# Parts of the output projection's operand in DRAM, and attention as one evenly spaced sequence with TensorE in source order

## The chip, the cores and the metric

The kernel runs on one core of a Trainium2 chip. The metric is the device time of one execution in microseconds (us), as the median of several runs. Profiles show one execution each; their times count from the start of its span.

The engines, as the profile names them: PE is TensorE (matmuls; PEld its weight loads), DVE is VectorE, ACT is ScalarE, POOL is GpSimd, SP is SyncE, which here only issues DMAs. ACT issues some DMAs and POOL issues others.

## What is computed

One block of a hybrid model on 512 tokens of width 2048, all in float32: a normalisation, one wide input projection, two mixers side by side (a state-space mixer, SSD, and a sparse attention with three branches), an output projection over both mixers' outputs, and a gated feed-forward net.

```python
u = rmsnorm(h, attn_norm_w)
z, xbc, dt, q, kc, vc, ks, vs, kw, vw, gate = split(u @ w_in)
y_ssd = rmsnorm(ssd(xbc, dt) * silu(z), ssd_norm_w)        # 1024 columns
# attention, 4 groups of 4 heads with 64 columns each; 1024 columns
o = g0 * softmax(q @ k_cmp) @ v_cmp                        # compressed branch
  + g1 * softmax(q_rot @ ks) @ vs + g2 * softmax(q_rot @ kw) @ vw
h = h + concat(y_ssd, o) @ w_out
h = h + (silu(n @ w_gate) * (n @ w_up)) @ w_down           # n = rmsnorm(h)
```

At 512 tokens both other branches reach over all earlier tokens, so the kernel computes them as two plain causal softmaxes with their own keys and values.

## The kernel before

All operands of matmuls are split into a high part in a short float format (`fp32r`) and a low part, the rest: `a_hi` makes the high part on ACT, `lo` the low part on DVE. A product takes three matmuls: high by high, high by low, low by high. Data stand transposed: features on the 128 partitions, the 512 tokens along the free dimension.

**Units.** Input and output projection are a list of units. A unit is one block of 128 output columns: it loads its weights in pieces of four k blocks (`raw` ring, SP's queue), splits them three pieces ahead (`whi` on ACT, `wlo` on DVE, rings of four), and runs three matmuls of 512 columns for each k block against the operand `U` (16 blocks of high parts, 16 of low parts), into `ps_g`. An input unit has 16 k blocks, an output unit 8 to 12: `NS` says how many, and the rest of the output projection is done later (the "oa" steps, lines 1184 to 1186). After its last matmul a unit's result is worked on by its evacuation, a generator `ev_...`.

**The order.** `Sched` holds generators. Each k block of a unit ends with `sch.tick()`, one step; `yield 3` in a generator means that it goes on three steps later. So everything that is not a projection (evacuations, attention, loads for the next stage) is written in between the units' matmuls, at distances counted in steps. `run_until` steps on without projection matmuls until a flag is set. From this source order the compiler makes each engine's own order: outside `manual_schedule` it may move instructions on TensorE ahead of or behind others by its own timing; inside, TensorE's instructions stay in source order. The other engines' order is the compiler's throughout. Before the change `manual_schedule` begins with the first unit of the output projection, `units[NU]`.

**Units of the second half of the input projection.** The z units (`U_Z`, eight; the evacuation multiplies the SSD mixer's result by silu(z) and stores the product in DRAM, `gy_d`), and for each attention group g the units VS, KS and two q units. Before, the order is VS0, KS0, Q00, Q01, Z4, Z5, VS1, KS1, Q10, Q11, Z6, VS2, KS2, Q20, Q21, Z7, VS3, KS3, Q30, Q31; then come the output units OUT0 to OUT15.

- `ev_vs` transposes the values on TensorE (line 698, tile `vt` into `ps_m`) and copies them into `v`, of which there are two; a third group waits until group g - 2 is finished, flag `("a", g - 2)`.
- `ev_ks` rotates the keys and makes `kh` and `kl`, two buffers each.
- `ev_q` makes `uq` (ACT and POOL), computes the compressed branch's scores (lines 776 and 777, into `ps_m`), and makes the rotated queries `rq`.
- `ps_m` is one PSUM bank, used by all of these in turn.

**Attention** is a generator of its own. For each group it waits for keys, values and both q units, does the compressed branch's softmax, and then goes through 32 items (4 heads, 2 branches, 4 blocks of queries). An item is `score` (two matmuls, a masked minimum on DVE, an exponential on ACT), `norm`, three items later `trans` (transposes, high and low parts `pth` and `ptl`), and after every fourth `pvmm`, the product with the values. An item takes one step and then `PACE` steps, 2.25 on the mean; from the output projection on `PACE_OUT`, 1.5. The first four blocks of 128 rows of attention's result are stored in DRAM as they are (`at_d`).

**Into the output projection.** The operand of the output projection takes the place of the input's in `U`. During the last input unit `ms_in` loads the SSD mixer's eight blocks from `gy_d`, multiplies them by the normalisation's row factor on POOL, and makes high and low part into `U`. At the first output unit `ma_in` loads attention's finished blocks, and splits them into `U`; the blocks that finish later are split into `U` directly. When attention is over, at the last output unit, `pre_oa` closes attention's pool and opens those of the next stage.

Of the kernel before, what the change touches and what calls it, by code (L numbers as in the profile page):

```python
# [29 lines left out]
PACE = [2,2,2,3]  # L30
PACE_OUT = [1,2,1,2]
LAG = 3
EB = 5
# [82 lines left out]
def body(ctx, tc, xT, w_in, w_out, w_gate, w_up, w_down, w1k, w1v, cols, rows, kst, out):  # L116
# [46 lines left out]
    at_d = dram.tile([8, 128, 512], F32, name="at_d")  # L163
# [384 lines left out]
    def ev_z(t):  # L548
        def ev(p):
# [33 lines left out]
    P2 = {}  # L583

# [103 lines left out]
    def ev_vs(g):  # L688
        def ev(p):
# [4 lines left out]
            yield 2  # L694
# [64 lines left out]
    def ev_q(g, j):  # L759
        def ev(p):  # L760
# [6 lines left out]
            yield 2  # L767
# [19 lines left out]
    def attention():  # L787
        yield from sch.wait("att", "cmp")
# [5 lines left out]
        for g in range(4):  # L794
            yield from sch.wait(("k", g), ("v", g), ("q", g, 0), ("q", g, 1))
            kh, kl = R["k", g]
            v = R["v", g]

            sc = R["sc", g]
            sm = ap.tile([128, 3, 4, 4], F32, tag="sm", name="sm", bufs=1)  # L800
            dve.tensor_reduce(sm[:, 0], sc, AX.X, ALU.max)
            dve.tensor_scalar(sm[:, 0], sm[:, 0], -1e20, None, op0=ALU.max)
            dve.tensor_tensor(sc.rearrange("p i h k -> p (i h) k"), sc.rearrange("p i h k -> p (i h) k"),
                              sm[:, 0].rearrange("p i h -> p (i h)")[:, :, None].to_broadcast([128, 16, 32]),
                              ALU.subtract)
            act.activation(sc, sc, AF.Exp, scale=0.125)
            for h in range(4):
                a_hi(vpad[32 * h:32 * h + 32, h, 0:64], vcmp[:, g, :])
                lo(dve, vpad[32 * h:32 * h + 32, h, 64:128], vcmp[:, g, :], vpad[32 * h:32 * h + 32, h, 0:64])
# [4 lines left out]
            mul(dve, sc.rearrange("p i h k -> p (i h) k"), sc.rearrange("p i h k -> p (i h) k"),  # L814
                sm[:, 2].rearrange("p i h -> p (i h)")[:, :, None].to_broadcast([128, 16, 32]))
            yield 6
            p = ps_t()
# [7 lines left out]
            yield 2  # L825

            items = [(h, br, i) for h in range(4) for br in range(2) for i in range(4)]
            pt, pr, po = {}, {}, {}

            def score(h, br, i):  # L830
                L = 128 * (i + 1)
                q = R["rq", g, h // 2][:, h % 2, i * 128:(i + 1) * 128]
                p = ps_s()
                pe.matmul(p[:, 0:L], q, kh[:, br, 0:L], start=True, stop=False)
                pe.matmul(p[:, 0:L], q, kl[:, br, 0:L], start=False, stop=True)
                e = ap.tile([128, 512], F32, tag="e", name="e", bufs=EB)
                m = ap.tile([128, 4], F32, tag="em", name="em", bufs=EB + 1)
                dve.tensor_tensor_reduce(e[:, 0:L], p[:, 0:L], kcs(K_AM + 512 - L, L), -0.125, 3e38,
                                         ALU.add, ALU.min, m[:, 0:1])
                act.activation(e[:, 0:L], e[:, 0:L], AF.Exp, scale=-1.0, bias=m[:, 0:1], accum_out=m[:, 1:2])  # L840
                pr[h, br, i] = (e, m)

            def norm(h, br, i):
                L = 128 * (i + 1)
                e, m = pr[h, br, i]
                gc = (4 * g + h) * 3 + 1 + br
                dve.reciprocal(m[:, 2:3], m[:, 1:2])
                if br:
                    dve.tensor_scalar(e[:, 0:L], e[:, 0:L], m[:, 2:3], gat[:, i, gc:gc + 1],
                                       op0=ALU.mult, op1=ALU.mult)  # L850
                else:
                    mul(dve, m[:, 3:4], m[:, 2:3], gat[:, i, gc:gc + 1])
                    a_hi(e[:, 0:L], e[:, 0:L], scale=m[:, 3:4])

            def trans(h, br, i):
                e, m = pr.pop((h, br, i))
                if i == 0:
                    pt[h, br] = (ap.tile([128, 13, 128], F32R, tag="pth", name="pth", bufs=2),
                                 ap.tile([128, 13, 128], F32R, tag="ptl", name="ptl", bufs=2))
                th, tl = pt[h, br]  # L860
                p = ps_t()
                for kb in range(i + 1):
                    pe.transpose(p[:, kb * 128:(kb + 1) * 128], e[:, kb * 128:(kb + 1) * 128], ident)
                s = p[:, 0:128 * (i + 1)].rearrange("p (a b) -> p a b", b=128)
                d = slice(i, 3 * i + i + 1, 3)
                a_hi(th[:, d, :], s)
                lo(dve, tl[:, d, :], s, th[:, d, :])

            def pvmm(h, br):
                th, tl = pt.pop((h, br))  # L870
                if br == 0:
                    o = po[h] = ps_v()
                    pe.matmul(o, vpad[:, h, :], ch, start=True, stop=False)
                    pe.matmul(o, vpad[:, h, :], cl, start=False, stop=False)
                o = po[h]
                for kb in range(4):
                    for t in (th, tl):
                        rhs = t[:, 4 * kb:3 * kb + 4, :].rearrange("p a b -> p (a b)")
                        pe.matmul(o[:, kb * 128:512], v[:, kb, br, :], rhs, start=False,
                                  stop=(br == 1 and kb == 3 and t is tl))  # L880
                if br == 1:
                    if h % 2 == 0:
                        R["at"] = ap.tile([128, 512], F32, tag="at", name="at", bufs=1)
                    at = R["at"]
                    a, b = (0, 64) if h % 2 == 0 else (64, 0)
                    fo = ap.tile([128, 512], F32, tag="fo", name="fo", bufs=1)
                    act.activation(fo[a:a + 64, :], o[b:b + 64, :], AF.Copy)
                    add(dve, at[a:a + 64, :], o[a:a + 64, :], fo[a:a + 64, :])
                    if h % 2:
                        k = 2 * g + h // 2  # L890
                        if "ma" in P2:
                            h_, l_ = P2["ma"][k]
                            a_hi(h_, at)
                            lo(dve, l_, at, h_)
                        else:
                            nc.gpsimd.dma_start(at_d[k], at)
                            P2["at"] = k
                        sch.flags.add(("at", k))

            n = len(items)  # L900
            for s in range(n + LAG + 1):
                if s < n:
                    score(*items[s])
                    if items[s][1:] == (1, 3):
                        sch.flags.add(("h", g, items[s][0]))
                yield 1
                if 0 <= s - LAG < n:
                    trans(*items[s - LAG])
                if s < n:
                    norm(*items[s])  # L910
                yield P2.get("pace", PACE)[s % len(PACE)]
                if 0 <= s - LAG - 1 < n and items[s - LAG - 1][2] == 3:
                    pvmm(*items[s - LAG - 1][:2])
            sch.flags.add(("a", g))
# [44 lines left out]
    def pre_ms():  # L959
        P2["ms"] = [(U[:, 0, k], U[:, 1, k]) for k in range(8)]  # L960
        sch.add(ms_in())

    def ms_in():
        assert "r2" in sch.flags
        for k in range(8):
            yield 2
            h_, l_ = P2["ms"][k]
            t = wp.tile([128, 512], F32, tag="raw", name="gy", bufs=4)
# [3 lines left out]
            dve.scalar_tensor_tensor(l_, t, col(C_SN + k), f(h_), op0=ALU.mult, op1=ALU.subtract)  # L972
            sch.flags.add(("ms", k))

    def pre_out():
        P2["pace"] = PACE_OUT
        sch.run_until(*[("gy", t) for t in range(8)])
        P2["ma"] = [(U[:, 0, 8 + k], U[:, 1, 8 + k]) for k in range(8)]
        sch.add(ma_in(P2["at"] + 1))

    def ma_in(n):

        for k in range(n):
            h_, l_ = P2["ma"][k]
# [4 lines left out]
            sch.flags.add(("ma", k))  # L989

    def ev_os(c):
        def ev(p):
            if c >= 12:
# [915 lines left out]
```

## Time and profile before

| | |
|---|---|
| three runs | 2238.38, 2241.39, 2245.98 us; median 2241.39 |
| the profiled execution | 2243.56 us, span 2241.8 us, mean granted clock of TensorE 0.986 |
| busy: PE, DVE, ACT, POOL | 97%, 80%, 53%, 19% of the span |
| second half of the input projection, from Q00's first matmul | 333.4 to 611.8 us |
| OUT0's first matmul | 631.8 us |
| attention's last matmul | 806.7 us |
| the end of the output units, and the first oa step | 823.3 us |

A row of the profile names the line of the code, the engine, the operation, the tiles written and read, the sizes, and how often; where time stands in brackets behind an arrow, the engine sat idle for that long before the instruction, and the arrow names what ended it. "PEclk" is the share of full speed that the throttle granted TensorE. Matmuls are pipelined, so the distance between two starts, not one's duration, is what a matmul costs.

### The profile page before, as it was taken

How to read it: one execution, taken by the hardware profiler on the slowest of the kernel's cores; microseconds unless marked ns; L12 is line 12 of the kernel's file. 1: busy time of each engine (PE TensorE's matmuls, PEld its weight loads, DVE VectorE, ACT ScalarE, POOL GpSimd, SP SyncE). 2: the span in 40 equal slices, each digit the busy share in tenths (PEclk: the TensorE clock that was granted, in tenths of full speed). 3: DMA queues.
4: the chain of work that ended last, by engine and by line, in shares of the span. 5: the costliest groups of instructions: out<-in, count | busy, mean ns of one | idle time of the engine just before them, and what ended most of it. 6: DMA issues, size and time to landing. Idle time of an engine off the chain costs nothing. (4 is left out here: it accounts for less than half of the span.)

```text
span 2241.8 us, 34995 instructions
## 1 busy us (share of the span) xinstructions
PE 2167.7 (97%) x12892; PEld 1908.6 (85%) x12892; DVE 1794.5 (80%) x2821; ACT 1196.4 (53%) x1991; POOL 432.3 (19%) x439
## 2 busy tenths in 40 slices
PE   7999999999999999999999999999999899999996
PEld 5888888888878887888888888888888889999996
DVE  7699766778886648988888888888887878888886
ACT  4564446666666657555555555555555333333453
POOL 2011225234331126000100000000000122221232
PEclk9999999999979999999999999999999999999998
DMA  5222343222334367788888788887878869686974
GB/s 179 90 71 76 120 151 100 76 83 69 97 88 116 104 189 226 223 222 251 227 228 235 219 249 231 239 235 214 249 218 268 315 197 307 191 283 183 298 184 135
DMA packets 170492, 416.66 MB, mean 186 GB/s; under 512 B 16800, under 2 KB 23984, under 8 KB 170320
## 3 DMA queue, kind: packets, MB, share of 16 engines
q1 hardware_dynamic: 98912, 246.73, 33.0%
q0 software_dynamic: 28112, 80.65, 18.4%
q10 hardware_dynamic: 43296, 87.04, 10.8%
q8 instruction: 101, 1.65, 0.3%
q14 instruction: 71, 0.58, 0.1%
HBM read 353.54 MB, written 57.15 MB: 183 GB/s over the span
## 5 line engine op out<-in xcount | busy, mean ns | idle before, releaser
L125 ACT ACTIVATE R<-Z 128x1024 fp32r<-128x1024 f32 (+4 forms) x458 | 415.5, 922 | 438.7 <-DVE Z L137 322.7
L128 DVE TENSOR_TENSOR R<-Z,R 128x1024 fp32r<-128x1024 f32 (+4 forms) x367 | 386.1, 1061 | 35.9 <-ACT R L125 21.1
L234 PE MATMUL ps_g<-u,whi 128*128 128x512 f32 x778 | 316.0, 406 | 0.0
L236 PE MATMUL ps_g<-u,wlo 128*128 128x512 f32 x778 | 307.7, 395 | 0.0
L235 PE MATMUL ps_g<-u,whi 128*128 128x512 f32 x778 | 306.3, 394 | 0.0
L1180 PE MATMUL ps_s<-u,R 128*128 128x512 f32 (+1 forms) x1160 | 252.9, 348 | 7.1 <-ACT A L1390 6.8
L128 DVE TENSOR_TENSOR wlo<-wraw,whi 128x512 fp32r<-128x512 f32 x211 | 159.5, 757 | 80.8 <-ACT whi L125 77.5
L1180 PEld LDWEIGHTS ps_s<-u,R 128*128 128x128 f32 x1160 | 187.7, 188 | 38.7 <-ACT A L1390 12.2
L125 ACT ACTIVATE whi<-wraw 128x512 fp32r<-128x512 f32 x211 | 131.9, 625 | 144.8 <-PE ps_g L235 98.6
L236 PEld LDWEIGHTS ps_g<-u,wlo 128*128 128x128 f32 x778 | 146.6, 188 | 30.6
L234 PEld LDWEIGHTS ps_g<-u,whi 128*128 128x128 f32 x778 | 147.0, 189 | 24.9 <-issue 0.2
L235 PEld LDWEIGHTS ps_g<-u,whi 128*128 128x128 f32 x778 | 147.1, 189 | 23.8
L1180 PE MATMUL ps_t<-u,R 128*128 128x512 f32 (+1 forms) x600 | 131.4, 347 | 0.0
L1180 PE MATMUL ps_g<-u,R 128*128 128x512 f32 x584 | 131.3, 349 | 0.0
L1180 PE MATMUL ps_s<-T,R 128*128 128x512 f32 (+1 forms) x560 | 125.7, 349 | 1.3 <-DVE R L128 1.3
L1180 PE MATMUL ps_g<-T,R 128*128 128x512 f32 (+1 forms) x584 | 125.7, 346 | 0.0
L1180 PE MATMUL ps_s<-V,R 128*128 128x512 f32 (+1 forms) x568 | 123.1, 347 | 0.0
L125 ACT ACTIVATE R<-A 128x1024 fp32r<-128x1024 f32 (+3 forms) x76 | 71.0, 934 | 86.3 <-DVE A L137 62.2
L137 DVE TENSOR_TENSOR Z<-Z 128x1024 f32<-128x1024 f32 (+5 forms) x96 | 106.1, 1105 | 8.8 <-POOL E L137 4.2
L137 DVE TENSOR_TENSOR A<-ps_g,A 128x512 f32<-128x512 f32 (+1 forms) x110 | 71.1, 653 | 51.5 <-PE ps_g L1180 38.6
L128 DVE TENSOR_TENSOR E<-Z,R 128x1024 fp32r<-128x1024 f32 (+1 forms) x91 | 109.9, 1208 | 1.5 <-ACT R L125 1.0
L1180 PEld LDWEIGHTS ps_t<-u,R 128*128 128x128 f32 x600 | 98.0, 188 | 14.1
(487 smaller groups left out, 5621.4 us busy)
## 6 DMA issues: line engine op xcount, KB each, us to landing
Z<-in_w_up SPq DMA_DIRECT2D x94, 512.0 KB, 5.3
Z<-in_w_gate SPq DMA_DIRECT2D x94, 512.0 KB, 6.4
wraw<-in_w_in SPq DMA_DIRECT2D x164, 256.0 KB, 2.5
g_d<-A ACTq DMA_DIRECT2D x22, 1792.0 KB, 15.0
Z<-in_w_up POOLq DMA_DIRECT2D x37, 512.0 KB, 8.9
Z<-in_w_gate POOLq DMA_DIRECT2D x37, 512.0 KB, 7.0
Z<-in_w_down SPq DMA_DIRECT2D x59, 320.0 KB, 5.7
Z<-in_w_down SPq DMA_DIRECT2D x41, 384.0 KB, 4.1
```

The lines of the kernel that those rows point to most:

```text
L125: act.activation(dst, src, AF.Copy, scale=scale)
L128: eng.tensor_tensor(dst, src, f(hi), ALU.subtract)
L137: eng.tensor_tensor(o, a, b, ALU.add)
L234: pe.matmul(p, hi_t[i][:, j, :], ah, start=(k == 0), stop=False)
L235: pe.matmul(p, hi_t[i][:, j, :], al, start=False, stop=False)
L236: pe.matmul(p, lo_t[i][:, j, :], ah, start=False, stop=(k == u.nk - 1))
L1180: pe.matmul(o, w, x, start=start, stop=(k == n - 1 and o is q), skip_group_check=not fresh[0])
```

## The change

- `PACE` is 2.125 steps on the mean, and `PACE_OUT` is gone. Attention is one sequence of 128 items over all groups, without a pause where a group begins. The compressed branch is a generator of its own, `compressed(g)`, started inside the group before.
- `manual_schedule` for TensorE begins at unit Z4, 16 units earlier than before; attention starts there (flag `"order"`).
- The order of units is VS0, KS0, Q00, Q01, Z4, VS1, KS1, Q10, Q11, Z5, Z6, Z7, VS2, KS2, Q20, Q21, VS3, KS3, Q30, Q31.
- In `ev_vs`, `ev_q` and after the last z unit the distances to the next work on TensorE are longer (2 to 6, 2 to 10, 0 to 12 steps).
- `ms_parts`, a new generator, makes high and low parts of the SSD mixer's blocks while the input projection runs, in slots of the `whi` and `wlo` rings, and stores both in DRAM (`gp_d`) through POOL's queue. `ms_in` then only loads them, 512 KB a block, into `U`. Attention's blocks 0 to 3 are split before their store in the same way, and `ma_in` only loads them.

```diff
-PACE = [2,2,2,3]
-PACE_OUT = [1,2,1,2]
+PACE = [2,2,2,2,2,2,2,3]
...
+                yield 12
                 P2["row2"] = sp.tile([128, 512], F32, tag="yz", name="row2", bufs=1)
-                sch.add(rms_stats(acc2, 1024, P2["row2"], "r2"))
+                sch.add(rms_stats(acc2, 1024, P2["row2"], "r2", gap=8))
+                sch.add(ms_parts())
...
+    def parts(dst, t, scale=None):
+        h = wp.tile([128, 512], F32R, tag="whi", name="hp", bufs=4)
+        l = wp.tile([128, 512], F32R, tag="wlo", name="lp", bufs=4)
...
+        nc.gpsimd.dma_start(dst[0], f(h))
+        nc.gpsimd.dma_start(dst[1], f(l))
+
+    def ms_parts():
+        yield from sch.wait("r2")
+        for k in range(8):
+            yield 8
+            t = wp.tile([128, 512], F32, tag="raw", name="gy", bufs=4)
+            nc.sync.dma_start(t, gy_d[k])
+            mul(pool, t, t, P2["row2"])
+            yield 2
+            parts(gp_d[k], t, col(C_SN + k))
+            sch.flags.add(("gp", k))
...
             mul(dve, t, p, rrow)            # ev_vs
-            yield 2
+            yield 6
...
             uq = q_stack(ap, "uq", 1, t, pool)
-            yield 2
+            yield 10
...
-        for g in range(4):
-            yield from sch.wait(("k", g), ("v", g), ("q", g, 0), ("q", g, 1))
...
+        def compressed(g):
+            yield from sch.wait(("q", g, 0), ("q", g, 1))
...
+            if g:
+                yield from sch.wait(("pv", g - 1, 3, 0))
             p = ps_t()
             for i in range(4):
                 pe.transpose(p[:, i * 128:(i + 1) * 128], sc[:, i].rearrange("p h k -> p (h k)"), ident)
...
+        items = [(g, h, br, i) for g in range(4) for h in range(4) for br in range(2) for i in range(4)]
+        n = len(items)
+        sch.add(compressed(0))
+        for s in range(n + LAG + 1):
+            if s < n:
+                g, h, br, i = items[s]
+                if (h, br, i) == (0, 0, 0):
+                    yield from sch.wait(("k", g), ("q", g, 0))
+                if (h, br, i) == (2, 0, 0):
+                    yield from sch.wait(("q", g, 1))
+                if (h, br, i) == (2, 0, 2) and g < 3:
+                    sch.add(compressed(g + 1))
+                score(*items[s])
...
+                if (h, br) == (0, 0):
+                    yield from sch.wait(("v", g), ("cc", g))
+                pvmm(g, h, br)
...
-        z = {0: [], 1: [4, 5], 2: [6], 3: [7]}[g]
+        z = {0: [], 1: [4], 2: [5, 6, 7], 3: []}[g]
...
     def pre_ms():
+        sch.run_until(("gp", 7))
         sch.add(ms_in())
...
-            nc.sync.dma_start(t, gy_d[k])
-            mul(pool, t, t, P2["row2"])
-            a_hi(h_, t, scale=col(C_SN + k))
-            dve.scalar_tensor_tensor(l_, t, col(C_SN + k), f(h_), op0=ALU.mult, op1=ALU.subtract)
+            nc.sync.dma_start(f(U[:, :, k, :]), gp_d[k].rearrange("s p t -> p s t"))
...
-            nc.sync.dma_start(f(l_), at_d[k])
-            yield 1 if k < 4 else 8
-            a_hi(h_, f(l_))
-            lo(dve, l_, f(l_), h_)
+            nc.sync.dma_start(f(U[:, :, 8 + k, :]), at_d[k].rearrange("s p t -> p s t"))
...
+    n_att = order.index(U_Z[4])
+    for n, u in enumerate(units[:n_att]):
...
     with tc.manual_schedule(engines={mybir.EngineType.PE}):
-        for u in units[NU:]:
+        sch.flags.add("order")
+        for u in units[n_att:]:
             run_unit(u)
```

More of the change, by code (lines that the diff above doesn't have):

```diff
@@ L162, in body @@
     y_d = dram.tile([4, 128, 512], F32, name="y_d")
-    at_d = dram.tile([8, 128, 512], F32, name="at_d")
+    at_d = dram.tile([8, 2, 128, 512], F32, name="at_d")
+    gp_d = dram.tile([8, 2, 128, 512], F32, name="gp_d")
     h1_d = dram.tile([KD, 128, 512], F32, name="h1_d")
@@ L787, in attention @@
     def attention():
-        yield from sch.wait("att", "cmp")
+        yield from sch.wait("att", "cmp", "order")
         ap = pools["att"][1]
@@ L813, in attention @@
             mul(dve, sm[:, 2], sm[:, 2], gat[:, :, 12 * g:12 * g + 12:3])
[L814 to L815 removed]
+            yield 2
+            mul(dve, rows, rows, wide(2))
             yield 6
+            if g:
+                yield from sch.wait(("pv", g - 1, 3, 0))
             p = ps_t()
@@ L825, in attention @@
             yield 2
[L827 to L905, printed above, removed]
-                yield 1
[L907 to L913, printed above, removed]
@@ L914, in attention, with score @@
-            sch.flags.add(("a", g))
+            for h in range(4):
+                a_hi(vpad[32 * h:32 * h + 32, h, 0:64], vcmp[:, g, :])
+                lo(dve, vpad[32 * h:32 * h + 32, h, 64:128], vcmp[:, g, :], vpad[32 * h:32 * h + 32, h, 0:64])
+                yield 1
+            yield 3
+            R["cc", g] = (ch, cl)
+            sch.flags.add(("cc", g))
+        pt, pr, po = {}, {}, {}
+        def score(g, h, br, i):
+            L = 128 * (i + 1)
+            q = R["rq", g, h // 2][:, h % 2, i * 128:(i + 1) * 128]
+            p = ps_s()
+            kh, kl = R["k", g]
+            pe.matmul(p[:, 0:L], q, kh[:, br, 0:L], start=True, stop=False)
+            pe.matmul(p[:, 0:L], q, kl[:, br, 0:L], start=False, stop=True)
+            e = ap.tile([128, 512], F32, tag="e", name="e", bufs=EB)
+            m = ap.tile([128, 4], F32, tag="em", name="em", bufs=EB + 1)
+            dve.tensor_tensor_reduce(e[:, 0:L], p[:, 0:L], kcs(K_AM + 512 - L, L), -0.125, 3e38,
+                                     ALU.add, ALU.min, m[:, 0:1])
+            act.activation(e[:, 0:L], e[:, 0:L], AF.Exp, scale=-1.0, bias=m[:, 0:1], accum_out=m[:, 1:2])
+            pr[g, h, br, i] = (e, m)
@@ new lines, in norm @@
+        def norm(g, h, br, i):
+            L = 128 * (i + 1)
+            e, m = pr[g, h, br, i]
+            gc = (4 * g + h) * 3 + 1 + br
+            dve.reciprocal(m[:, 2:3], m[:, 1:2])
+            if br:
+                dve.tensor_scalar(e[:, 0:L], e[:, 0:L], m[:, 2:3], gat[:, i, gc:gc + 1],
+                                   op0=ALU.mult, op1=ALU.mult)
+            else:
+                mul(dve, m[:, 3:4], m[:, 2:3], gat[:, i, gc:gc + 1])
+                a_hi(e[:, 0:L], e[:, 0:L], scale=m[:, 3:4])
@@ new lines, in trans @@
+        def trans(g, h, br, i):
+            e, m = pr.pop((g, h, br, i))
+            if i == 0:
+                pt[g, h, br] = (ap.tile([128, 13, 128], F32R, tag="pth", name="pth", bufs=2),
+                             ap.tile([128, 13, 128], F32R, tag="ptl", name="ptl", bufs=2))
+            th, tl = pt[g, h, br]
+            p = ps_t()
+            for kb in range(i + 1):
+                pe.transpose(p[:, kb * 128:(kb + 1) * 128], e[:, kb * 128:(kb + 1) * 128], ident)
+            s = p[:, 0:128 * (i + 1)].rearrange("p (a b) -> p a b", b=128)
+            d = slice(i, 3 * i + i + 1, 3)
+            a_hi(th[:, d, :], s)
+            lo(dve, tl[:, d, :], s, th[:, d, :])
@@ new lines, in pvmm @@
+        def pvmm(g, h, br):
+            th, tl = pt.pop((g, h, br))
+            if br == 0:
+                ch, cl = R["cc", g]
+                o = po[h] = ps_v()
+                pe.matmul(o, vpad[:, h, :], ch, start=True, stop=False)
+                pe.matmul(o, vpad[:, h, :], cl, start=False, stop=False)
+            o = po[h]
+            v = R["v", g]
+            for kb in range(4):
+                for t in (th, tl):
+                    rhs = t[:, 4 * kb:3 * kb + 4, :].rearrange("p a b -> p (a b)")
+                    pe.matmul(o[:, kb * 128:512], v[:, kb, br, :], rhs, start=False,
+                              stop=(br == 1 and kb == 3 and t is tl))
+            if br == 1:
+                if h % 2 == 0:
+                    R["at"] = ap.tile([128, 512], F32, tag="at", name="at", bufs=1)
+                at = R["at"]
+                a, b = (0, 64) if h % 2 == 0 else (64, 0)
+                fo = ap.tile([128, 512], F32, tag="fo", name="fo", bufs=1)
+                act.activation(fo[a:a + 64, :], o[b:b + 64, :], AF.Copy)
+                add(dve, at[a:a + 64, :], o[a:a + 64, :], fo[a:a + 64, :])
+                if h % 2:
+                    k = 2 * g + h // 2
+                    if "ma" in P2:
+                        h_, l_ = P2["ma"][k]
+                        a_hi(h_, at)
+                        lo(dve, l_, at, h_)
+                    else:
+                        parts(at_d[k], at)
+                        P2["at"] = k
+                    sch.flags.add(("at", k))
@@ L1809, in body @@
     units[0].evac = ev_first
-    for n, u in enumerate(units):
+    n_att = order.index(U_Z[4])
+    for n, u in enumerate(units[:n_att]):
         if n == 4:
```

41 lines of the change are left out of this document (26 added, 15 removed).

## The prediction

> **What bounds the kernel now.** I read the page's busy times and slices first, then busy time by stretch, then TensorE's order of time around the one stretch that stands out, then the tiles that it waits on there.
>
> ```profile
> PE 2167.7 (97%) x12892; PEld 1908.6 (85%) x12892; DVE 1794.5 (80%) x2821; ACT 1196.4 (53%) x1991; POOL 432.3 (19%) x439
> PE   7999999999999999999999999999999899999996
> PEclk9999999999979999999999999999999999999998
> ```
>
> TensorE is the bound: 97% busy, and the one slice inside the program where its granted clock falls (the twelfth, 616 to 672 us) is the place that this change touches. So the question is where TensorE waits or runs slowly between the second half of the input projection and the end of the output projection, since the change adds and removes no matmul.
>
> ```profile
> core 0: us, PE busy (x) PEld busy (x) DVE busy (x) ACT busy (x) POOL busy (x), PEclk, DMA share, GB/s
> 333.40:611.80 278.40, 277.93 (x1448) 236.17 (x1447) 207.56 (x523) 182.38 (x408) 102.95 (x105) 1.00 0.26 84
> 611.80:631.80 20.00, 14.42 (x65) 12.59 (x63) 19.82 (x36) 12.43 (x28) 15.39 (x16) 0.65 0.30 93
> 631.80:655.00 23.20, 20.52 (x89) 16.50 (x89) 20.62 (x57) 14.59 (x35) 4.66 (x4) 0.79 0.28 80
> 655.00:806.80 151.80, 151.80 (x792) 127.50 (x791) 98.26 (x294) 95.59 (x233) 17.23 (x24) 1.00 0.39 105
> 806.80:823.30 16.50, 16.50 (x76) 13.66 (x75) 5.03 (x8) 6.51 (x11) 2.30 (x3) 1.00 0.84 265
> ```
>
> The reader sees five stages: input projection with attention (the compiler orders TensorE there), its end, the start of the output projection, the rest of it (TensorE already in source order), and its last unit after attention has ended. The first stage and the last two leave TensorE nothing: 277.93 busy of 278.40, 151.80 of 151.80, 16.50 of 16.50, all at clock 1.00. Only the middle 43.2 us are bad: 14.42 + 20.52 = 34.94 us busy, at 0.65 and 0.79 of the clock.
>
> ```profile
> 612.45 0.51 PE L863 MATMUL ps_t<-ident,e 128*128 128x128 f32 x3
> 616.16 0.50 PE L834 MATMUL ps_s<-kh,rq 128*128 128x512 f32 x1 [3.20 <-DVE em L838]
> 619.49 0.38 PE L776 MATMUL ps_m<-kch,uq 128*128 128x32 f32 x1
> 628.75 0.39 PE L776 MATMUL ps_m<-kch,uq 128*128 128x32 f32 x1 [1.23 <-POOL uq L128]
> 631.76 0.77 PE L234 MATMUL ps_g<-u,whi 128*128 128x512 f32 x1
> 632.33 0.63 PE L235 MATMUL ps_g<-u,whi 128*128 128x512 f32 x1
> 632.76 0.63 PE L236 MATMUL ps_g<-u,wlo 128*128 128x512 f32 x1
> L698 PE MATMUL ps_m<-ident,vt x16: 270/272/322, 333.3 to 579.0; 128*128 128x128 f32 x16
> 617.80 0.39 ACT L125 ACTIVATE v<-ps_m 128x256 fp32r<-128x256 f32 x1 [0.46 <-DVE v L128]
> ```
>
> Between 612 and 631.76 no projection matmul runs: TensorE has only the end of attention group 1 and the scores of the last two q units. Those scores (L776) start late because `ps_m` has one buffer: VS3's transposes filled it by 579, and its copy into `v` waits for one of two `v` buffers, which group 1's last pv frees only at 612. So the copy ends at about 618, and L776 follows at 619.49. The reason is lag: counted in the code from Z4's first step (one step is one k of a unit), group 1 ends at step 255, while VS3's evacuation starts at 208. In source order 31 steps of attention, and later 8, then stand alone with no projection beside them.
>
> **The change, part by part.**
>
> *1. The lag goes.* One sequence at 2.125 + 1 = 3.125 steps an item, with no pause at a group's start, ends group 1 at (64 + 4) x 3.125 + 10 (the wait for the first compressed result), about step 223; group 3 ends at 423, and OUT15 starts at 439. VS3's unit stays at steps 192 to 208; its transposes are asked for at 208 + 6 = 214 (210 before), nine steps ahead of group 1's end instead of 45, and the scores of q(3,0), at step 240 + 10 = 250, find `ps_m` free. No stretch without projection matmuls is left. Worth: the 43.2 us hold 14.42 x 0.65 + 20.52 x 0.79 = 25.6 us of work at full clock, so 17.6 us are to be had, 8.3 as idle time and 9.3 as slow clock. I take all of it: -17.6. The low end is the idle time alone, -8.3, if other waits keep the clock down.
>
> The slow clock is in the rows: 0.43 us from L235 to L236 at 632.33, against 0.23 below. The Trainium skill, TensorE: Matmul & The Clock Gate, Part 1, says that an idle window of about 3.4 us halves the clock until about 3.4 us of work have passed. By that rule a wait costs at most 1.7 us of clock, and three such waits here would make the part 8.3 + 5.1 = 13.4; the rows show more, and I keep 17.6.
>
> *2. TensorE in source order from Z4 on.* Nothing on TensorE is added; what may be added is waiting, because a late operand now holds up everything behind it.
>
> ```profile
> 653.39 0.39 PE L873 MATMUL ps_v<-cph,vpad 128*128 128x512 f32 x1
> 675.00 0.39 PE L873 MATMUL ps_v<-cph,vpad 128*128 128x512 f32 x1
> 609.06 0.39 PE L235 MATMUL ps_g<-u,whi 128*128 128x512 f32 x1
> 609.74 0.39 PE L235 MATMUL ps_g<-u,whi 128*128 128x512 f32 x1
> 866.99 0.39 PE L1186 MATMUL ps_g<-u,E 128*128 128x512 f32 x1
> 870.50 0.79 PE L1184 MATMUL ps_g<-u,R 128*128 128x512 f32 x1 [3.11 <-DVE A L137]
> 871.09 0.63 PE L1185 MATMUL ps_g<-u,R 128*128 128x512 f32 x1
> 873.65 0.47 PE L1185 MATMUL ps_g<-u,R 128*128 128x512 f32 x1
> ```
>
> Source order alone costs nothing where it stands already: 655 to 806.8 has no idle time, at a denser spacing than the new one (a head of 8 items in 21.6 us, of which 20 steps of 0.68 are projection, so 1 us of attention an item and 2.7 us from item to item; afterwards 3.125 x 0.68 + 1 = 3.1). But VectorE is at 98.26/151.8 = 65% there. In the input projection it is at 207.56/278.4 = 75%, and 77 items instead of 68 by its end bring that to about 80%. So it lies between 0 and, as the dense stretch shows, 8.3 us of idle time in 43 us, which over 256 us would be 49. It is nearer to the first, since what made the second (no projection matmuls between) is gone. I take one wait as at 870.50 (3.1 us, then seven matmuls in 3.15 us instead of 1.6): +4.7.
>
> *3. The hi and lo parts by way of DRAM.* Per block k of the SSD half: one multiplication on POOL, one copy on ACT, one subtraction on DVE, as before, but spread over steps 150 to 228 instead of crowding the 43 us.
>
> ```profile
> L134 POOL TENSOR_TENSOR gy<-gy,row x8: 1275/1302/1754, 602.7 to 631.6; 128x512 f32<-128x512 f32 x8
> L125 ACT ACTIVATE u<-gy,colc x8: 707/716/726, 606.0 to 633.3; 128x512 fp32r<-128x512 f32 x8
> L972 DVE SCALAR_TENSOR_TENSOR u<-gy,colc,u x8: 730/746/1395, 606.8 to 636.4; 128x512 fp32r<-128x512 f32 x8
> L896 POOL DMA_DIRECT2D at_d<-at x4: 586/590/618, 443.7 to 619.8; - x4
> 602.72 2.56 POOL L134 TENSOR_TENSOR gy<-gy,row 128x512 f32<-128x512 f32 x2
> 602.89 1.14 DVE L134 TENSOR_TENSOR em<-em,gat 128x1 f32<-128x1 f32 x1
> 598.39 0.16 DVE L134 TENSOR_TENSOR em<-em,gat 128x1 f32<-128x1 f32 x1
> ```
>
> That is 8 x 1.3 us of POOL, 8 x 0.72 of ACT and 8 x 0.75 of DVE moved into a stretch where these are 37, 66 and 75% busy: 0, hidden behind TensorE; without that cover 22 us. The attention blocks 0 to 3 are split before the store instead of after the load, by the same two operations: 0. New are 16 + 4 more DMA issues on POOL, 20 x 0.59 = 12 us: POOL is idle for 175 of 278 us, so 0, with the rival below for what queues behind them. The parts take slots of the `whi` and `wlo` rings, so the next weights are split one block of 4 steps later, with two blocks (8 x 0.68 = 5.4 us and some attention) still ahead: 0.
>
> A POOL operation that reads SBUF holds up a two-input DVE one: 1.14 us instead of 0.16 beside the multiplications at 602.72. The Trainium skill, SBUF — State Buffer, "SBUF: two separate sides", calls this an exclusive lock held for the whole instruction. The trace agrees; by it the eight multiplications block DVE for up to 10.4 us wherever they stand, and the sum stays if DVE's idle quarter takes them.
>
> *4. Loads into `U`.* SP reads 12 blocks of 512 KB instead of 256 KB, straight into `U`, behind the matmuls of the last unit that read it. Blocks 0 to 10 are needed by step 11 of OUT0: 5.8 MB, with 1.8 MB of weights, from the start of Q31, some 30 us (27 steps and 9 items). That is 250 GB/s; the row of 806.8 to 823.3 shows 265 at a DMA share of 0.84. So it just fits. Bounds 0 and 5 us (5.8 + 1.8 MB at 265 GB/s is 28.7 us, plus a landing and a slow restart); I take +1.
>
> *5. Behind it.* Attention ends 439 - 423 = 16 steps ahead of OUT15, 20 before: the pool that waits for it opens at most 2.7 us later relative to TensorE, in a stretch with 11 us of TensorE work between (806.8 to OUT15). 0. The 3.1 us wait at 870.50 stays.
>
> Sum: -17.6 + 4.7 + 1 = -11.9. The profiled execution took 2243.6 us (span 2241.8), 2.2 above the median of 2241.4; against the profiled execution that is 2231.7, against the median, which I forecast, 2229.5, in round numbers 2229.
>
> **The rivals.**
>
> *Full gain.* Source order costs nothing in the new stretch either, as in 655 to 806.8, and the loads are in time: -18, and -21 to -24 if the restart at 870.50 falls otherwise: 2217 to 2223. For it: not 1 us of idle in the source-ordered stage. Against it: VectorE 15 points busier.
>
> *Given back.* The 256 us of input projection wait as much as the dense stretch loses now: within 7 us of 2241. That takes 13 to 20 us, 5 to 8% of that stretch, or 0.2 us an item; ptl, the last link before pv, has 5 steps (3.4 us and an item) for a copy, a subtraction and what is queued on DVE ahead of them.
>
> *Slower.* POOL becomes the late engine, and L776 waits for it in source order, at six q units.
>
> ```profile
> 596.47 0.67 DVE L134 TENSOR_TENSOR qt<-ps_g,rrow 128x512 f32<-128x512 f32 x1
> 597.44 0.52 POOL L715 DMA_DIRECT2D sw<-qt  x1 [3.57 <-DVE qt L134]
> 599.52 3.12 POOL L128 TENSOR_TENSOR uq<-qt,uq 64x512 fp32r<-64x512 f32 x2
> ```
>
> From qt to the end of uq it is 602.64 - 596.47 = 6.2 us; the new ten steps with three items cover 9.8. A pair of parts ahead of it on POOL adds 1.3 + 2 x 0.59 and a wait for DVE, some 3 to 4: 9.2 to 10.2, just covered. It turns the sign where each of the six comes 3 us late (17.6/6), a chain of 12.8; at 15 us it is 6 x (5.2 + 1.6) = 41 us, less 17.6: 2265. The Trainium skill, TensorE: Matmul & The Clock Gate, Part 2, says that only weight loads are pulled ahead and matmuls stay in program order, so there is no way round a late one; the 3.20 us at 616.16 agree. Against it: L776 waited only 1.23 us for uq even in the crowded stretch.
>
> **How the numbers follow.** What can be told from no change here is 0.3%, 6.7 us. Forecast (-7 to -17): 0.50. Full gain (-17 to -26): 0.18. Given back (within 6.7): 0.18. Slower: 0.14. Faster 0.68, same 0.18, slower 0.14. The likeliest time is 2229, its own range 2221 to 2235; the range, with both neighbours, 2215 (-26) to 2248 (+6.7), leaves out the slower case and a little below, under 2 in 10.
>
> **What would show it.** Right: no stretch between Z4 and OUT15 with the clock under 0.95 and no gap of TensorE over 2 us at the first output unit; L698 of VS3 followed by its copy within 2 us; group 3's last pv 8 to 12 us ahead of OUT15; everything behind 823 as long as before. Wrong: idle time of TensorE in the input projection above 5 us with PE waits for ptl, em or uq (part 2 or the slower rival); a wait of OUT0 for a DMA into `u` (part 4); or a longer stretch behind 823, which I have at nothing.

## Result and profile after

| | before | after |
|---|---|---|
| median of 5 runs each, side by side | 2243.47 us (2238.38 to 2246.58) | 2231.89 us (2230.45 to 2233.11) |
| ratio | 1 | 0.9946, 95% interval 0.9933 to 0.9960 |
| profiled execution, span | 2243.56, 2241.8 us | 2233.11, 2231.3 us |
| first oa step | 823.3 us | 813.3 us |
| feed-forward net, first matmul of its kind `ps_s<-u,R` | 902.6 us | 892.7 us |

The change makes the kernel 0.54% faster. From the first oa step on nothing moves: from there to the net it is 79.3 us before and 79.4 after, and from the net to the end of the span 1339.2 and 1338.6. So the gain lies ahead of 813 us. The page of the changed kernel, busy times and the clock by slices:

```profile
PE 2158.5 (97%) x12892; PEld 1897.8 (85%) x12892; DVE 1793.7 (80%) x2821; ACT 1195.4 (54%) x1991; POOL 438.9 (20%) x459
PEclk8999999999999999999999999999999999999998
```

The 7 in the twelfth slice of the clock is a 9 now; the 8 at the start is a difference between profiled executions far from the change. TensorE's busy sum fell by 9.2 us with the same 12892 matmuls, since "busy" includes matmuls at a low clock. By stretches (length; PE, PEld, DVE, ACT, POOL busy, with instructions; clock; DMA share; GB/s), and TensorE's waits from 334 to 830 us in the same kernel (what was waited for; us in total, times, longest):

```profile
334.50:600.00 265.50, 259.69 (x1358) 216.91 (x1357) 207.21 (x518) 178.22 (x402) 103.38 (x113) 1.00 0.29 97
600.00:625.00 25.00, 24.91 (x133) 20.73 (x132) 23.30 (x55) 18.38 (x44) 16.14 (x19) 1.00 0.56 185
625.00:650.00 25.00, 25.00 (x139) 21.18 (x138) 22.66 (x55) 15.63 (x39) 10.73 (x11) 1.00 0.77 267
618.00:798.40 180.40, 180.40 (x943) 151.60 (x942) 125.01 (x353) 112.80 (x274) 33.42 (x42) 1.00 0.48 144
```

```profile
PE ps_t L895 <- DVE ptl L127: 1.6, 2, 0.9
PE ps_t L844 <- DVE ptl L127: 1.6, 2, 1.4
PE ps_v L913 <- DVE ptl L127: 1.4, 3, 0.5
PE ps_v L913 <- ACT pth L124: 1.3, 1, 1.3
```

The stretch at 0.65 and 0.79 of the clock is gone: from 618 to 798.4 us TensorE has no idle time at all. In its place stand 5.8 us of idle time in the input projection (265.50 - 259.69), where there were 0.5 (the first row of stretches in the prediction), in short waits, the longest 1.4 us by this list. The clock stays at 1.00. The kernel before, by the same stretches:

```profile
600.00:625.00 25.00, 20.66 (x103) 17.39 (x102) 23.33 (x49) 18.16 (x41) 15.17 (x15) 0.86 0.41 129
625.00:650.00 25.00, 21.09 (x92) 17.89 (x92) 23.21 (x56) 14.88 (x37) 10.64 (x8) 0.70 0.33 94
650.00:675.00 25.00, 25.00 (x127) 20.75 (x126) 18.63 (x57) 17.46 (x44) 2.02 (x3) 0.96 0.30 85
```

Below, "lost" is the length of a stretch less busy time times granted clock. From 600 to 675 us it is 18.5 us before (7.2 + 10.2 + 1.0) and 0.1 after.

The table "Time and profile before" needs a correction. OUT0's first two k blocks ran at 609.5 to 611.6 us, ahead of the gap (the row at 609.74 in the prediction is one of them); 631.8 us is its third. In source order that third block stood behind the scores of q(3,1), and these behind the scores of q(3,0).

### The profile page after: what moved, and what is told of

Its sections match the earlier page's. It is cut to its first block, busy times and chain, and to the rows that moved or that the text cites. A ratio compares the mean times of both kernels' runs of the same rounds, so it can differ in the third digit from the quotient of the medians.

```text
span 2231.3 us, 35003 instructions
## 1 busy us (share of the span) xinstructions
PE 2158.5 (97%) x12892; PEld 1897.8 (85%) x12892; DVE 1793.7 (80%) x2821; ACT 1195.4 (54%) x1991; POOL 438.9 (20%) x459
## 5 line engine op out<-in xcount | busy, mean ns | idle before, releaser
L127 DVE TENSOR_TENSOR R<-Z,R 128x1024 fp32r<-128x1024 f32 (+4 forms) x367 | 380.8, 1046 | 30.8 <-ACT R L124 19.6
L872 ACT ACTIVATE e<-e,em 128x128 f32<-128x128 f32 (+3 forms) x128 | 71.6, 559 | 76.1 <-DVE em L870 75.5
```

Of the source, the lines that this page charges most:

```text
L127: eng.tensor_tensor(dst, src, f(hi), ALU.subtract)
```

## Experiments

Each kernel was timed in five rounds against the kernel before on the same chip. A cell of the first table is the ratio to before.

| TensorE from Z4 on | SSD parts | attention as before | attention even |
|---|---|---|---|
| compiler's order | at the transition | 1 (before) | 1.0013 [1.0000, 1.0025] |
| compiler's order | through DRAM | 1.0074 [1.0055, 1.0093] | 0.9996 [0.9982, 1.0009] |
| source order | at the transition | 1.0100 [1.0080, 1.0120] | 1.0014 [1.0002, 1.0025] |
| source order | through DRAM | 1.0053 [1.0035, 1.0071] | 0.9946 [0.9933, 0.9960] (after) |

No part alone, and no two of them, make the kernel faster. The cells are not alike in everything else: all but the two with the compiler's order and attention as before have the change's order of units, its longer pauses, and attention's blocks 0 to 3 split before their store. What these do was not tested apart.

Theory L (the prediction's) was that the lag of attention makes the slow stretch, and that the even spacing removes it. Theory S was that TensorE's order does. Theory C was crowding: that making the SSD mixer's parts at the transition holds TensorE up.

### Even attention and parts in DRAM, TensorE in the compiler's order

```diff
-    for n, u in enumerate(units[:n_att]):
+    for n, u in enumerate(units[:NU]):
+        if n == n_att:
+            sch.flags.add("order")
...
     with tc.manual_schedule(engines={mybir.EngineType.PE}):
-        sch.flags.add("order")
-        for u in units[n_att:]:
+        for u in units[NU:]:
```

> The changed kernel, but TensorE in source order only from the first output unit on, as before. Theory L (attention's lag behind the projection, and ps_m held by VS3's transposes because of it, made the stretch of 612 to 655 us; source order only adds waits, seven of them with some 6 us in the changed kernel): the stretch stays gone without source order, and the compiler avoids most of the seven waits: 12 to 18 us under the kernel before, 2225 to 2231. Rival S (source order itself cured the stretch, since the compiler no longer moves VS3's transposes ahead): the stretch comes back, clock under 0.9 near the first output unit, 0 to 4 us under the kernel before.

Measured: 2243.92 us, ratio 0.9996. The stretch is back. First the windows of this kernel (all instructions), then, for the projection's matmuls of line 234 alone (one for each k block; PE and PEld, clock, DMA share, GB/s), this kernel and the changed one:

```profile
600.00:625.00 25.00, 18.68 (x85) 14.42 (x84) 20.52 (x47) 16.61 (x39) 13.95 (x15) 0.86 0.44 140
625.00:650.00 25.00, 21.64 (x108) 18.09 (x107) 17.85 (x42) 12.10 (x30) 10.91 (x10) 0.86 0.75 271
```

```profile
580.00:600.00 20.00, 8.23 (x21) 3.83 (x21) 1.00 0.52 170
600.00:620.00 20.00, 3.58 (x8) 1.90 (x8) 0.84 0.30 91
620.00:640.00 20.00, 7.46 (x18) 3.25 (x18) 0.99 1.03 376
```

```profile
580.00:600.00 20.00, 6.91 (x16) 3.08 (x16) 1.00 0.41 134
600.00:620.00 20.00, 8.55 (x21) 3.77 (x20) 1.00 0.45 151
620.00:640.00 20.00, 7.38 (x18) 3.40 (x18) 1.00 1.04 363
```

The compiler takes projection matmuls ahead of attention's: 21 k blocks in 580 to 600, and then only 8 are left for the 20 us ahead of the boundary, where source order has 16 and 21. Attention then stands with too little beside it and waits for VectorE, as in the rows of TensorE's order of time:

```profile
576.95 0.66 PE L723 MATMUL ps_m<-ident,vt 128*128 128x128 f32 x4 [0.71 <-DVE vt L133]
612.34 0.50 PE L866 MATMUL ps_s<-kh,rq 128*128 128x512 f32 x1 [2.59 <-DVE em L870]
615.91 0.58 PE L866 MATMUL ps_s<-kh,rq 128*128 128x256 f32 x1 [1.60 <-DVE em L870]
618.00 0.63 PE L235 MATMUL ps_g<-u,whi 128*128 128x512 f32 x1
618.43 0.63 PE L236 MATMUL ps_g<-u,wlo 128*128 128x512 f32 x1
625.65 0.18 PE L801 MATMUL ps_m<-kch,uq 128*128 128x32 f32 x1
642.67 0.79 PE L913 MATMUL ps_v<-ptl,v 128*128 128x512 f32 x1 [3.34 <-DVE ptl L127]
```

The rows at 618 show the low clock: 0.43 us from one matmul to the next, where 0.23 is usual. The wait at 642.67 lies in the output projection, where TensorE is in source order; why `ptl` was late there stays open.

VS3's copy into `v` here ended on VectorE at 606.2, so `ps_m` was free 19 us ahead of q(3,0)'s scores at 625.65, and the stretch loses 15.3 us all the same. So `ps_m` is not what holds this one; freeing it alone in the kernel before was not tried. The lag itself is not gone: VS3's transposes run at 576.95, and their copy waits for group 1 until 600.01, 23 us (36 before, 2.4 in the changed kernel). Even spacing in the source is thus not even on TensorE while the compiler may move projection matmuls ahead. Theory L's remedy is not sufficient by itself; the outcome is rival S's.

### Attention faster, nothing else

```diff
-PACE = [2,2,2,3]
+PACE = [2,2,2,1]
```

> The kernel before with one number changed: PACE [2,2,2,1], 2.75 steps an item instead of 3.25, so that group 1 ends about step 219 from Z4 instead of 255, nine steps after VS3's evacuation starts. Theory L (lag): most of the stretch goes, 8 to 16 us under the kernel before, 2227 to 2235. Rival C (crowding: the SSD parts made at the transition on POOL, ACT and DVE are what holds TensorE up there): the stretch stays, 0 to 4 us under it.

Measured: 2247.64 us, ratio 1.0010 [0.9999, 1.0020].

```profile
600.00:625.00 25.00, 20.13 (x92) 16.39 (x90) 22.73 (x33) 14.83 (x34) 16.67 (x16) 0.82 0.39 127
625.00:650.00 25.00, 20.56 (x79) 16.38 (x79) 24.42 (x48) 13.14 (x29) 13.83 (x9) 0.63 0.20 66
```

```profile
618.59 0.36 PE L776 MATMUL ps_m<-kch,uq 128*128 128x32 f32 x1 [1.00 <-DVE v L128]
```

A faster pace gains nothing, but it also took little of the lag away. Group 1's last product with `v`, the one just ahead of VS3's copy, starts at 606.39 us, where it stood at 612.34 before: 6 us, not the 36 steps of the source. VS3's copy into `v` starts at 608.95, still 34 us behind its transposes at 575.0 (36 us before), and the scores of q(3,0) still wait for it, at 618.59. So this experiment does not decide on theory L. VectorE is busy for 24.42 of 25 us in the slow stretch.

### Parts through DRAM, nothing else

The generator `ms_parts` and the loads of the change, in the kernel before, with its own order of units. Z7 comes late there, so the parts must be made in the last units, and the loads wait for them (`run_until`).

> The kernel before with the SSD mixer's high and low parts made during the input projection and brought in through DRAM, as in the change; attention, order of units and TensorE's order as before. Theory L (lag): VS3's copy still waits for group 1, the stretch stays, 0 to 4 us under the kernel before. Rival C (crowding): 9 to 13 us under it.

Measured: 2263.89 us, ratio 1.0074: 17 us slower, which neither theory expected. The window, TensorE's longest wait in it, and ScalarE's order of time ahead of that wait:

```profile
600.00:625.00 25.00, 14.84 (x55) 12.01 (x54) 16.47 (x48) 14.00 (x34) 8.24 (x11) 0.57 0.38 121
```

```profile
621.53 0.80 PE L235 MATMUL ps_g<-u,whi 128*128 128x512 f32 x1 [6.37 <-ACT whi L125]
```

```profile
620.24 0.72 ACT L125 ACTIVATE hp<-gy,colc 128x512 fp32r<-128x512 f32 x1 [4.76 <-POOL gy L134]
620.87 1.66 ACT L125 ACTIVATE whi<-wraw 128x512 fp32r<-128x512 f32 x3
```

The wait of 6.37 us is that of the unit before the last of the input projection (Q30), for the `whi` of its last piece. On ScalarE this `whi` stands behind the high part of an SSD block (`hp`), which had waited 4.76 us for its multiplication on POOL. From 591 to 621.5 us no projection matmul runs at all. In the change Z7 stands a group earlier, so this cell is the parts without the room that the change makes for them.

### Even attention and source order, the parts at the transition

```diff
-                sch.add(ms_parts())
...
-        sch.run_until(("gp", 7))
...
-            nc.sync.dma_start(f(U[:, :, k, :]), gp_d[k].rearrange("s p t -> p s t"))
+            h_, l_ = P2["ms"][k]
+            t = wp.tile([128, 512], F32, tag="raw", name="gy", bufs=4)
+            nc.sync.dma_start(t, gy_d[k])
+            mul(pool, t, t, P2["row2"])
+            a_hi(h_, t, scale=col(C_SN + k))
+            dve.scalar_tensor_tensor(l_, t, col(C_SN + k), f(h_), op0=ALU.mult, op1=ALU.subtract)
```

> The changed kernel with the SSD mixer's parts made at the transition again, as before (load, POOL, ACT, DVE, no gp_d). Theory L (lag): within 3 us of the changed kernel, 2229 to 2235. Rival C (crowding): a wait at the first output unit and a lower clock there, 6 to 12 us over the changed kernel.

Measured: 2248.68 us, ratio 1.0014. The window, and the largest entry in the list of TensorE's waits in 600 to 680:

```profile
625.00:650.00 25.00, 13.90 (x51) 9.53 (x50) 19.90 (x32) 11.28 (x23) 17.89 (x16) 0.73 0.52 169
```

```profile
PE ps_g L235 <- DVE u L1018: 8.4, 5, 3.5
```

TensorE's first matmuls of the output projection wait five times for low parts of `U`, made behind a multiplication on POOL of 1.3 us or more each; 14.9 us are lost in these 25. The part that the prediction held to be worth nothing is worth 15 us once the two others are in place. That is rival C's outcome, and more than its 6 to 12 us.

### Parts in DRAM and source order, attention as before

```diff
-PACE = [2,2,2,2,2,2,2,3]
+PACE = [2,2,2,3]
+PACE_OUT = [1,2,1,2]
...
-        def compressed(g):
-            yield from sch.wait(("q", g, 0), ("q", g, 1))
+        for g in range(4):
+            yield from sch.wait(("k", g), ("v", g), ("q", g, 0), ("q", g, 1))
...
```

> The changed kernel (parts by way of DRAM, TensorE in source order from Z4 on), with the attention generator of before: group by group, eight items close together at a group's head, a pause at its start, PACE [2,2,2,3]. Lag theory (what is left of the prediction's part 1): group 1 ends 30 steps later again, its last 31 steps of attention stand without projection beside them, in source order, so the granted clock falls below 0.9 somewhere in 600 to 680 us: 8 to 15 us over the changed kernel, ratio to before 0.998 to 1.001. Rival (source order and the parts are what counts, the even spacing is worth nothing): within 3 us of the changed kernel, ratio 0.994 to 0.996, and the clock at 0.98 or more all through.

Measured: 2256.07 us, ratio 1.0053, some 24 us more than the changed kernel's 0.9946. The window of attention's lag, and TensorE's longest waits in it:

```profile
585.00:612.00 27.00, 15.99 (x59) 12.14 (x58) 22.44 (x57) 16.55 (x43) 11.99 (x14) 0.68 0.26 89
```

```profile
PE ps_t L889 <- DVE ptl L128: 4.3, 4, 1.9
PE ps_s L860 <- DVE em L864: 2.9, 1, 2.9
```

Here the lag does what the prediction said it would do in source order: attention stands alone (no projection matmul runs in this window), waits for VectorE link by link, and the clock falls to 0.68. These 27 us lose 27 - 15.99 x 0.68 = 16.1; the window 650 to 675 loses 5.2 more. The lag theory's direction held; its 8 to 15 us were too few, and the stretch came earlier than its 600 to 680 us.

### Even attention alone, and source order alone

Both complete the table; the diffs are those above.

> The even attention alone: TensorE in source order only from the first output unit on, and the hi and lo parts of the SSD half made between the projections, as before. It completes the table of the three parts. If the three act only together: within 0.3% of before (0.997 to 1.003). If the parts by way of DRAM do harm while TensorE's order is the compiler's, as they did to the kernel before (ratio 1.0074): this one comes out 5 to 15 us below the changed kernel with that order (which was 0.9996), so 0.993 to 0.997. If the even attention does harm alone: above 1.003.

> Source order alone: the kernel before with TensorE in source order from Z4 on (with the order of units and the pauses in the q units that go with it), but with its own attention and with the SSD half's parts made between the projections. It is the last cell of the table. If the three causes of the slow stretch lie over one another and any one of them keeps it (so far: with one part missing 1.0053, 0.9996, 1.0014 of before): 1.003 to 1.012, with the bare attention of the version with old attention (waits of its transposes at 585 to 611 us) and the waits of the output's first unit for the low parts of U. If source order by itself is what frees the stretch: 0.994 to 0.998.

Measured: 2246.60 us, ratio 1.0013, and 2268.88 us (2262.38 to 2274.59), ratio 1.0100, the slowest of all. A window of the first, which also waits for low parts of `U` (4.0 us in three waits); then windows of the second, and its wait for high parts of `U`:

```profile
625.00:650.00 25.00, 16.81 (x67) 12.72 (x66) 19.67 (x32) 13.52 (x28) 19.66 (x16) 0.84 0.36 117
```

```profile
585.00:612.00 27.00, 19.70 (x85) 15.12 (x84) 18.07 (x46) 16.14 (x39) 6.26 (x6) 0.81 0.06 21
625.00:650.00 25.00, 18.33 (x89) 14.26 (x87) 21.83 (x43) 14.61 (x35) 17.08 (x16) 0.83 0.58 179
650.00:675.00 25.00, 21.12 (x91) 16.75 (x91) 19.86 (x50) 13.54 (x32) 6.63 (x6) 0.77 0.30 85
```

```profile
PE ps_g L235 <- ACT u L125: 5.9, 3, 3.9
```

Source order without the rest has the bare attention of one experiment at 585 and the late parts of the other at 625, one behind the other: TensorE can't go round either. The start of the feed-forward net moves about as the ratios do: 927.3 us here, 919.7 with the parts alone, 916.6, 907.4, 907.2 and 903.9 with two parts or even attention alone, 902.6 before, 892.7 after.

### What the remaining idle time hangs on

The kernel after, as the one before, loads tables on ScalarE where the SiLU of a z unit comes between attention's exponentials. Below are the groups of ScalarE's loads in 300 to 800 us, and ScalarE's order of time ahead of TensorE's first wait, which stands in the last fence, a row of TensorE's order:

```profile
L872 ACT ACT_TABLE_LOAD x5 | 6.4, 1283 | 0.1
L568 ACT ACT_TABLE_LOAD x4 | 5.1, 1283 | 0.1
```

```profile
374.89 1.28 ACT L568 ACT_TABLE_LOAD   x1
376.19 0.63 ACT L568 ACTIVATE zs<-zs 128x512 f32<-128x512 f32 x1
376.73 0.47 ACT L124 ACTIVATE pth<-ps_t 128x384 fp32r<-128x384 f32 x1
377.22 1.28 ACT L872 ACT_TABLE_LOAD   x1
378.51 0.51 ACT L872 ACTIVATE e<-e,em 128x256 f32<-128x256 f32 x1
```

```profile
383.30 0.66 PE L844 MATMUL ps_t<-ident,sc 128*128 128x128 f32 x4 [1.44 <-DVE ptl L127]
```

Three experiments: the changed kernel with the product with v ("pv") one item later, without the SiLU, and with the SiLU by tanh.

```diff
-        for s in range(n + LAG + 1):
+        for s in range(n + LAG + 2):
...
-            if 0 <= s - LAG - 1 < n and items[s - LAG - 1][3] == 3:
+            if 0 <= s - LAG - 2 < n and items[s - LAG - 2][3] == 3:
...
```

> The changed kernel with the product with v one item later (3 steps more between the transposes and pv). Theory (TensorE's 5.9 us of idle time in the input projection is mostly pv waiting for a copy or subtraction that stands behind others on VectorE): the waits of pv for ptl and pth go, 2 to 4 us less than the changed kernel. Rival (VectorE is late as a whole; what pv no longer waits for, the transposes and scores wait for): within 1.5 us of the changed kernel, with the waits at the transposes instead, or 1 to 3 us more because attention ends 3 steps later.

Measured: 2232.43 us, ratio 0.9944 [0.9927, 0.9960]: as the changed kernel. pv no longer waits (2.7 us by the list above), and the transposes (L844, L895) wait 5.4 us from 334 to 830 us instead of 3.2: the rival.

```diff
-                act.activation(zs, zs, AF.Silu)
+                act.activation(zs, zs, AF.Copy)
```

> The changed kernel without the SiLU of z units 4 to 7 (a plain copy stands in its place, so the gate is left out of the result). Table theory: each SiLU among attention's exponentials costs two table loads of 1.28 us on ScalarE, and they are what makes TensorE wait at 381 and 465 us (1.83 and 1.11 us): eight loads fewer in the input projection, both waits gone, 2 to 4 us less than the changed kernel. Rival (the waits come from VectorE's queue, the loads lie in ScalarE's idle time): within 1.5 us of the changed kernel, the idle time of TensorE there still 5 to 6 us.

Measured: 2228.12 us, ratio 0.9928 [0.9910, 0.9947]. Idle time up to 600 us is 2.9 us instead of 5.8, and the two waits that the expectation names, which end at 383.30 and 466.69 us in the changed kernel, are gone. That is the table theory's outcome, though the interval overlaps that of the changed kernel.

```diff
-                mul(dve, zs, p, rrow)
-                act.activation(zs, zs, AF.Silu)
+                dve.scalar_tensor_tensor(zs, p, 0.5, rrow, op0=ALU.mult, op1=ALU.mult)
+                th = sp.tile([128, 512], F32, tag="qs", name="th", bufs=2)
+                act.activation(th, zs, AF.Tanh)
+                dve.scalar_tensor_tensor(zs, th, 1.0, zs, op0=ALU.add, op1=ALU.mult)
```

> The changed kernel with the SiLU of z units 4 to 7 computed as h + h tanh(h), h = z/2: tanh on ScalarE, one operation more on VectorE (about 0.73 us) a unit; the result is the same function. Theory (the table loads are what the version without SiLU saved): if tanh and the exponential need no load between them, the nine loads in 300 to 800 us become one and the time falls by 3 to 4 us, ratio to before 0.992 to 0.994. Rival (tanh needs loads as SiLU did): no loads fewer, and the extra operations add 0 to 2 us, 0.994 to 0.996.

> The changed kernel once more, on the same chip as the version with tanh and source order alone, for a comparison side by side: 0.9933 to 0.996 of before, nine table loads in 300 to 800 us, TensorE idle for 5 to 7 us in the input projection.

Measured, on one chip: with tanh 2229.48 us (2227.39 to 2231.10), ratio 0.9930 [0.9918, 0.9942]; the changed kernel again 2235.62 us (2228.38 to 2238.60), ratio 0.9955 [0.9942, 0.9968]. The version with tanh, its loads, its input projection, and the net's first matmul (889.3 us; 893.8 in the changed kernel timed beside it):

```profile
L874 ACT ACT_TABLE_LOAD x1 | 1.3, 1283 | 0.0
```

```profile
334.50:600.00 265.50, 262.44 (x1369) 220.57 (x1368) 212.87 (x527) 170.80 (x398) 105.87 (x117) 0.99 0.30 98
```

```profile
L1221 PE MATMUL ps_s<-u,R x1160: 277/391/511, 889.3 to 1733.8; 128*128 128x512 f32 x174, 128*128 128x256 f32 x20
```

One load is left of nine, idle time is 3.1 us instead of 6.0, and the net begins 4.5 us earlier (3.4 earlier than in the first profile of the changed kernel). The medians differ by 6.1 us; what goes beyond the idle time is not explained. This version is faster than the kernel before. Against the changed kernel its median is lower, and the two intervals touch at 0.9942.

## Why the prediction came out, and where its steps failed

The forecast was 2229 us against 2241.4, a ratio of 0.9945; measured was 0.9946, 2231.89 us against 2243.47. The sum of -11.9 us is met (-11.6), but not by its reasons: it credits even spacing with a gain that all three parts bring only together, and it is in part luck that the change had all three. By the two profiles the first oa step comes 10.0 us earlier, less than the two large terms as measured below (-18.4 and 5.3); 1.1 us of the difference is a later start of Q00 (334.5 us, 333.4 before), and the rest, 2 us, is within what the rounding of the clock to 0.01 leaves open over 480 us.

- **Term 1, the lag (-17.6).** The size is right: 600 to 675 us lost 18.5 us before and 0.1 after. The attribution failed, at "The reason is lag". Even attention alone gains nothing (1.0013), and with the parts in DRAM nothing either (0.9996). That `ps_m` holds the scores of the last q units is right for the kernel before, but with even attention and parts in DRAM in the compiler's order it was free 19 us ahead of them, and the stretch stayed. Three causes lay in the same 60 us: attention that falls behind in the source, a compiler's order that takes projection matmuls away from it, and the making of `U`'s parts. With one of them left in place 15 to 22 us are lost there (15.3, 15.6 and, from 585 us on, 21.5), so what each earns can't be added up. Even attention is worth 24 us, but only where the two others are done.
- **Term 2, source order (+4.7).** As idle time in the input projection 5.3 to 5.5 us, so the size is right, as many short waits and not one long one. The Trainium skill, TensorE: Matmul & The Clock Gate, Part 1, halves the clock behind an idle window of about 3.4 us. The waits of up to 1.4 us here left the clock at 1.00, which agrees. The version with even attention and parts in DRAM in the compiler's order does not agree: the longest wait shortly ahead of its matmuls at 618 us is 2.59 us, and they start 0.43 us apart instead of 0.23, so shorter waits were enough. The term took source order for a cost alone. With the other two parts in place it earns 11 us (0.9996 to 0.9946); without them, with the order of units that goes with it, it costs 22 (1.0100).
- **Term 3, the parts (0).** Failed: what they cost where they stood was put down to the lag, and with the other two in place it is 15 us. They were costed only where they went, and there they are nearly hidden: with the parts at the transition the input projection's idle time is 3.7 us (265.50 - 261.85), with them in it 5.8. So some 2 us of term 2's size are theirs.
- **Term 4, the loads into `U` (+1).** Nothing: no wait of OUT0 for a DMA. The changed kernel's twelve loads, with their time to landing (least, median, most):

```profile
L1015 SPq DMA_DIRECT2D u<-gp_d x8: 359/438/1138, 617.5 to 625.4; - x8
L1026 SPq DMA_DIRECT2D u<-at_d x4: 359/360/360, 628.7 to 632.1; - x4
DMA to landing us min/median/max: 5.4/9.5/10.7
```

- **Term 5 (0).** As said. The wait of 3.11 us at 870.50 is 3.43 us at 860.86 in the trace after. One count is off: by the units' k blocks (256 of the input projection, then 11 + 11 + 13 x 12) OUT15 starts at step 434, not 439. So attention ends 12 steps ahead of it, not 16; nothing hung on it.
- **What was to show it.** VS3's transposes, which start at 596.64 and end at 597.3, are followed by the copy into `v` at 599.04; no stretch shown has a clock under 0.95; group 3's last pv at 799.50 is 8.4 us ahead of OUT15's first matmul at 807.86: as said. The sign against it, idle time of TensorE over 5 us with waits for `ptl`, came true as well, and it was paid for in the sum.
- **The rivals.** Full gain fell short by the input projection's idle time; the version with tanh gets half of that back. "Given back" did not happen. For "Slower" nothing waited for `uq` in the trace after.

## What to carry to other kernels

Where several delays lie over one another in one place, the time lost there is set by whichever is left, so take the parts of a change away one at a time before any of them is credited with the whole, and don't be surprised when each part alone gains nothing. Source order on TensorE paid here only where everything it can no longer go round was on time: even spacing of the dependent chain and operands made well ahead come first. A function of another table between a chain's exponentials cost a load each way; writing it in terms of a function that needs no load cost one VectorE operation more a unit.

## What the runs showed of the hardware

- A change of ScalarE's table took 1283 ns, nine times in this stage, with 0.1 us of idle time in all in front of each of the two groups. The Trainium skill, ScalarE: Activation LUTs, "Table sets: the hidden batching unit", has tanh in the set of exp; the trace agrees, since the loads between them are gone. The section "What ACT_TABLE_LOAD costs" gives about 2.66 us for a switch with its drain; here the function started right behind the 1.28 us (374.89 to 376.19).
- While the loads into `U` ran, the core's DMAs moved 363 GB/s in all (620 to 640 us above), more than the 265 GB/s that the prediction took for a bound.
- TensorE's clock fell to about half behind a wait of 2.59 us and, 2.0 us after it, one of 1.60 us (the rows from 612.34 to 618.43 above).
